# Part of a modulation's column sums moved from VectorE to GpSimd in a one-core transformer kernel

## The chip, the cores and the metric

The kernel runs on one core of a Trainium2 chip. The metric is device microseconds (us) of one execution; lower is better. Three timed runs of the kernel before gave 2441.3, 2444.15 and 2444.39 us, so the median is 2444.15 us.

## The reference, cut to what matters

The reference is three transformer layers on a 256 x 2048 float32 activation. Only the first layer is modulated by a conditioning vector `c` of 2048 numbers:

```
mod = (c @ w_mod + b_mod).reshape(6, 2048)        # w_mod is 2048 x 12288, float32
shift_m, scale_m, gate_m, shift_f, scale_f, gate_f = mod
h    = rms_norm(x, g_pre_mix) * (1 + scale_m) + shift_m
proj = h @ w_in                                    # and so on: mixing, w_out
x    = x + gate_m * rms_norm(mix_out, g_post_mix)
h2   = rms_norm(x, g_pre_ffn) * (1 + scale_f) + shift_f
...
x    = x + gate_f * rms_norm(f, g_post_ffn)
```

The other matrix products are split into a high and a low part in a reduced format (three matmuls for each). The product `c @ w_mod` is different: it is one row times a 100 MB matrix, so it costs little arithmetic and much reading.

## The kernel before, in words

**Weights of the large products.** All matrices come in 1024 KB loads into three buffers `raw`, issued by SyncE's queue (line 130). Each half of a load, 128 x 1024, is split: ScalarE rounds it to `wh` (line 134), VectorE subtracts, `wl = raw - wh` (line 135), and TensorE multiplies with both. There are three `wh` and three `wl` buffers. This happens 802 times and is most of VectorE's work. Both inputs of line 135 lie in SBUF.

**The modulation** is summed over `c`'s 16 chunks of 128 rows. For each chunk, 128 rows of `w_mod` lie on the 128 partitions, and VectorE does `acc = w * c_k + acc` with `c_k` one number per partition (`scalar_tensor_tensor`; the first chunk only multiplies, `tensor_scalar`). At the end TensorE adds the 128 partitions up with a column of ones. It is done in two ways.

*First part: scale_m and shift_m, in `start` (lines 756 to 898).* They are needed before `h` exists. The first 256 columns are done in `first`. The rest goes in four groups (`steps`): columns of chunks 2-3, 4-7, 8-11 and 12-15, that is 256, 512, 512 and 512 columns. For a group, loads of 1024 KB (`raws`, line 769) alternate between scale (segment 1) and shift (segment 0); a load holds 8 chunks of 256 columns or 4 chunks of 512. `mod_part` (lines 777 and 779) adds it up in `macc[:, 0]` (scale) or `macc[:, 1]` (shift). There are three `raws` buffers used in turn, so a load waits until the load three places before it has been used. When both sums are there, TensorE's line 793 adds up the partitions, VectorE's line 800 adds the bias, and lines 808 to 810 make the next chunks of `h` (`xh`, `xl`). `run` weaves the groups into the products with the chunks of `h` that are already there (`pairs(0)`, `pairs(2)`, `full(1)`, `full(2)`), so that a group's chunks are ready two pieces of work before their turn.

*The rest: gate_m, scale_f, shift_f and gate_f, in `mod_tile` (line 446).* It takes tiles of one chunk by 1024 columns (512 KB, line 453, two or three buffers), 96 in the attention block and 32 in the FFN. VectorE's line 457 (first chunk) or 460 adds each in `mac`; the sum over partitions (line 442, by `mod_flush`) is made when the next run of 16 tiles is at its second tile. `side` hands the tiles out at a rate of 3, later 4, for each load of weights.

**What orders the work.** Each engine works through its own list in order. The framework makes the lists at build time from priorities and from its own timing of each instruction. SyncE's queue issues the `raw`, `raws` and `rawm` loads in one list, so a load that waits for its buffer holds up those behind it. GpSimd does almost nothing: sixteen powers of at most two columns and a few small loads.

Of the kernel before, what the change touches and what calls it, by code (L numbers as in the profile page):

```python
# [12 lines left out]
ALU = mybir.AluOpType  # L13
# [3 lines left out]
P = 128  # L17
T = 256
D = 2048
KC = D // P  # L20
# [69 lines left out]
class Kern:  # L90
# [51 lines left out]
    def mm3(self, out, ah, al, bh, bl, start, stop):  # L142
        mm = self.nc.tensor.matmul
        mm(out, ah, bh, start=start, stop=False, skip_group_check=True)  # L144
        mm(out, ah, bl, start=False, stop=False, skip_group_check=True)  # L145
        mm(out, al, bh, start=False, stop=stop, skip_group_check=True)  # L146
# [299 lines left out]
    def mod_tile(self, new, at, k):  # L446

        nc = self.nc

        if k == 1:  # L450
            self.mod_flush()
        raw = new("rawm")
        nc.sync.dma_start(raw, self.A["w_mod"][k * P:(k + 1) * P, at * P:(at + 8) * P])
        cc = self.vcol("c", k)
        if k == 0:
            self.mac = new("mac")
            nc.vector.tensor_scalar(self.mac, raw, cc, None, ALU.mult)
        else:
            dst = self.mac if k < KC - 1 else raw
            nc.vector.scalar_tensor_tensor(dst, raw, cc, self.mac, ALU.mult, ALU.add)  # L460
        if k == KC - 1:
            self.mod_due = (raw, 8, at)

# [292 lines left out]
    def start(self, ps, low, xs, xl, X, sbs, cst):  # L756
        nc, A = self.nc, self.A
# [8 lines left out]
        def mod_load(seg, c0, n, k0, nk):  # L766
            raws.append(raws.pop(0))
            raw = raws[-1]().rearrange("p (k n) -> p k n", k=nk)
            nc.sync.dma_start(raw, wm[:, k0:k0 + nk, seg * D + c0:seg * D + c0 + n])
            return raw  # L770

        def mod_part(acc, raw, k0, n=None):

            for k in range(n or raw.shape[1]):
                cc = self.vcol("c", k0 + k)
                if k0 + k == 0:
                    nc.vector.tensor_scalar(acc, raw[:, k], cc, None, ALU.mult)
                else:
                    nc.vector.scalar_tensor_tensor(acc, raw[:, k], cc, acc, ALU.mult, ALU.add)

        def steps(j0, n):

            macc = ps.tile([P, 2, 512], F32, name="macc", tag="macc", bufs=2)
            nk = 16 // n
            for q in range(0, KC, nk):
                for i, seg in enumerate((1, 0)):
                    mod_part(macc[:, i, :n * P], mod_load(seg, j0 * P, n * P, q, nk), q)
                    yield None
            mp = self.acc("b")
            for i in range(2):  # L790
                for j in range(n):
                    o = i * n + j
                    nc.tensor.matmul(mp[:, o:o + 1], macc[:, i, j * P:(j + 1) * P], self.ones1,
                                     start=o == 0, stop=o == 2 * n - 1, skip_group_check=True)
            yield mp
# [24 lines left out]
        def first():  # L820

            mp = self.acc("b")
            macc = ps.tile([P, 2, 512], F32, name="macc", tag="macc", bufs=2)
            for q in range(0, KC, 8):
                for i, seg in enumerate((1, 0)):
                    if i:
                        raw = self.wp.tile([P, 2048], F32, name="raw", tag="raw", bufs=RAW).rearrange("p (k n) -> p k n", k=8)
                        nc.sync.dma_start(raw, wm[:, q:q + 8, seg * D:seg * D + 2 * P])
                    else:
                        raw = mod_load(seg, 0, 2 * P, q, 8)  # L830
                    mod_part(macc[:, i, :2 * P], raw, q, 6)
                    for k in range(6, 8):
                        for j in range(2):
                            o = 2 * i + j
                            nc.tensor.matmul(mp[:, o:o + 1], raw[:, k, j * P:(j + 1) * P], self.vcol("c", q + k),
                                             start=q + k == 6 and o == 0, stop=False, skip_group_check=True)
            for o in range(4):
                nc.tensor.matmul(mp[:, o:o + 1], macc[:, o // 2, o % 2 * P:(o % 2 + 1) * P], self.ones1,
                                 start=False, stop=o == 3, skip_group_check=True)
            return mp  # L840
# [38 lines left out]
        def run(work, nw, j0, n, lead=2):  # L879

            s = steps(j0, n)
            nm = 2 * n
            done = 0
            for i, _ in enumerate(work):
                while done < nm and done * (nw - lead) < (i + 1) * nm:
                    next(s)
                    done += 1
                if done == nm:
                    chunks(j0, n, next(s))
                    done += 1  # L890
# [582 lines left out]
```

## Time and profile before

| | |
|---|---|
| timed runs, median (lowest, highest) | 2444.15 us (2441.3, 2444.39) |
| profiled execution, its own time | 2438.1 us |
| its span, first to last instruction | 2436.1 us |
| TensorE busy | 2378.1 us, 98% |
| VectorE busy | 1678.5 us, 69% |
| ScalarE busy | 1246.7 us, 51% |
| GpSimd busy | 19.3 us, 1% |

Busy time is the time in which at least one instruction of the engine was in progress. Matmul records are pipelined and their ends are modelled, so TensorE's share says only that it seldom waited. In the views below a stretch is given in us from the span's start; "xN" counts instructions; "idle before" is time the engine stood still just before such instructions, with what released it. `PE` is TensorE, `PEld` its weight loads, `DVE` VectorE, `ACT` ScalarE, `POOL` GpSimd, `SPq` SyncE's queue.

### The profile page before, as it was taken

To read this page: it belongs to the slowest core of one execution; us is meant where nothing else is said; L and a number is where in the kernel's file an instruction comes from. 1 tells how busy PE (TensorE), PEld (TensorE's weight loads), DVE (VectorE), ACT (ScalarE), POOL (GpSimd) and SP (SyncE) were. 2 spreads that over 40 slices of the span, in tenths; PEclk is the share of its full clock that TensorE was granted. 3 is DMA by queue.
4 is the path that set the end of the run, shared out by engine and by line. 5 is a ranking of instruction groups with operands and counts; after the bars stand their busy time and mean duration, and the time that the engine had idled before them with its cause. 6 is when DMAs were issued, how large, how long until landed. Compare 5 with 4: busy or idle time off the path is not lost.

```text
span 2436.1 us, 37172 instructions
## 1 busy us (share of the span) xinstructions
PE 2378.1 (98%) x15142; PEld 2153.9 (88%) x15142; DVE 1678.5 (69%) x2213; ACT 1246.7 (51%) x1716; POOL 19.3 (1%) x30
## 2 busy tenths in 40 slices
PE   7999999999989999999999989999999999999997
PEld 6899989999868888888888879998898899999986
DVE  8997898888777575555556566756664477777764
ACT  5877674534464444444445454445644455554543
POOL 0000000000000000000000000000000000000000
PEclk9999999999999999999999999999999999999999
DMA  9997557999948585555555545555655544454453
GB/s 365 349 365 259 182 177 272 329 350 333 350 161 321 191 291 193 190 189 187 194 197 200 190 149 191 191 189 186 228 193 190 190 163 167 158 189 169 161 190 138
DMA packets 104043, 540.61 MB, mean 222 GB/s; under 512 B 9888, under 2 KB 18240, under 8 KB 53184
## 3 DMA queue, kind: packets, MB, share of 16 engines
q1 hardware_dynamic: 100896, 526.19, 60.8%
q10 hardware_dynamic: 2160, 8.88, 1.0%
q0 software_dynamic: 816, 3.16, 0.4%
q8 instruction: 118, 1.93, 0.3%
q14 instruction: 53, 0.43, 0.1%
HBM read 533.99 MB, written 4.21 MB: 221 GB/s over the span
## 4 chain that ended last, share of the span: by engine, by line
PE 94%; DVE 2%; ACT 1%; DMA 1%; issue 1%; POOL 0%; SPq 0%; DVEq 0%; POOLq 0%
PE acca L145 15%; PE acca L144 15%; PE acca L146 15%; PE acca L212 11%; PE acca L211 11%; PE acca L213 11%; PE acca L193 2%; PE acca L194 2%; PE acca L192 2%; PE accb L212 2%; PE accb L213 2%; PE accb L211 2%; DMA hid<-in_w_mod_dram 1%; DVE wl L135 1%; PE accb L1343 1%
## 5 line engine op out<-in xcount | busy, mean ns | idle before, releaser
L135 DVE TENSOR_TENSOR wl<-raw,wh 128x1024 fp32r<-128x1024 f32 x802 | 977.9, 1221 | 570.9 <-ACT wh L134 568.3
L134 ACT CAST wh<-raw 128x1024 fp32r<-128x1024 f32 x802 | 841.7, 1051 | 864.0 <-PE acca L213 377.9
L145 PE MATMUL acca<-Ql,wh 128*128 128x256 f32 x1024 | 290.5, 284 | 0.0
L144 PE MATMUL acca<-Qh,wh 128*128 128x256 f32 x1024 | 289.8, 284 | 0.0
L146 PE MATMUL acca<-Qh,wl 128*128 128x256 f32 x1024 | 285.5, 281 | 0.0
L212 PE MATMUL acca<-wl,Fh 128*128 128x512 f32 x704 | 276.8, 393 | 1.0 <-DVE wl L135 0.9
L213 PE MATMUL acca<-wh,Fl 128*128 128x512 f32 x704 | 275.7, 393 | 0.3 <-DVE Fl L716 0.3
L211 PE MATMUL acca<-wh,Fh 128*128 128x512 f32 x704 | 252.3, 396 | 1.7 <-ACT Fh L714 1.7
L144 PE MATMUL acca<-xh,wh 128*128 128x256 f32 x832 | 232.8, 284 | 4.5 <-ACT xh L808 3.4
L145 PE MATMUL acca<-xl,wh 128*128 128x256 f32 x832 | 233.7, 284 | 0.0
L146 PE MATMUL acca<-xh,wl 128*128 128x256 f32 x832 | 227.0, 283 | 0.0
L144 PEld LDWEIGHTS acca<-Qh,wh 128*128 128x128 f32 x1024 | 192.9, 188 | 0.5
L145 PEld LDWEIGHTS acca<-Ql,wh 128*128 128x128 f32 x1024 | 192.6, 188 | 0.8
L146 PEld LDWEIGHTS acca<-Qh,wl 128*128 128x128 f32 x1024 | 192.1, 189 | 0.4
L144 PEld LDWEIGHTS acca<-xh,wh 128*128 128x128 f32 x832 | 158.1, 190 | 7.3 <-ACT xh L808 3.6
L145 PEld LDWEIGHTS acca<-xl,wh 128*128 128x128 f32 x832 | 157.4, 189 | 1.6 <-issue 0.7
L212 PEld LDWEIGHTS acca<-wl,Fh 128*128 128x128 f32 x704 | 132.7, 189 | 29.1 <-DVE wl L135 2.2
L211 PEld LDWEIGHTS acca<-wh,Fh 128*128 128x128 f32 x704 | 131.3, 188 | 30.0 <-ACT Fh L714 2.9
L213 PEld LDWEIGHTS acca<-wh,Fl 128*128 128x128 f32 x704 | 132.4, 188 | 28.6 <-DVE Fl L716 1.5
L146 PEld LDWEIGHTS acca<-xh,wl 128*128 128x128 f32 x832 | 155.1, 190 | 1.3 <-issue 1.0
L145 PE MATMUL acca<-Al,wh 128*128 128x256 f32 x512 | 143.7, 282 | 0.0
L144 PE MATMUL acca<-Ah,wh 128*128 128x256 f32 x512 | 142.7, 281 | 0.0
(374 smaller groups left out, 4600.5 us busy)
## 6 DMA issues: line engine op xcount, KB each, us to landing
raw<-in_w_fgu_dram SPq DMA_DIRECT2D x88, 1024.0 KB, 4.8
raw<-in_w_inb_dram SPq DMA_DIRECT2D x64, 1024.0 KB, 4.8
raw<-in_w_in_dram SPq DMA_DIRECT2D x51, 1024.0 KB, 6.3
rawm<-in_w_mod_dram SPq DMA_DIRECT2D x96, 512.0 KB, 5.7
raw<-in_w_fd_dram SPq DMA_DIRECT2D x44, 1024.0 KB, 4.8
raw<-in_w_ina_dram SPq DMA_DIRECT2D x32, 1024.0 KB, 4.8
raws<-in_w_mod_dram SPq DMA_DIRECT2D x30, 1024.0 KB, 8.4
raw<-in_w_in_g_dram SPq DMA_DIRECT2D x16, 1024.0 KB, 7.2
```

The costliest lines, as they stand in the source:

```text
L134: nc.scalar.copy(wh[:, :per], raw[:, a:a + per])
L135: nc.vector.tensor_sub(wl[:, :per], raw[:, a:a + per], wh[:, :per].bitcast(F32))
L144: mm(out, ah, bh, start=start, stop=False, skip_group_check=True)
L145: mm(out, ah, bl, start=False, stop=False, skip_group_check=True)
L146: mm(out, al, bh, start=False, stop=stop, skip_group_check=True)
L192: mm(banks[h], xh[:, t], wh[:, s], start=fresh and k == 0, stop=False, skip_group_check=True)
L193: mm(banks[h], xh[:, t], wl[:, s], start=False, stop=False, skip_group_check=True)
L194: mm(banks[h], xl[:, t], wh[:, s], start=False, stop=k == nk - 1, skip_group_check=True)
L211: mm(banks[h][q], xh[:, t], wh[:, w], start=k == 0, stop=False, skip_group_check=True)
L212: mm(banks[h][q], xh[:, t], wl[:, w], start=False, stop=False, skip_group_check=True)
L213: mm(banks[h][q], xl[:, t], wh[:, w], start=False, stop=k == nk - 1, skip_group_check=True)
L1343: nc.tensor.matmul(ps[:, g * T:(g + 1) * T], q[g][:, P:T], kT, start=g == 0, stop=g == 1, skip_group_check=True)
```

## The change

In `steps` the scale stays with `mod_part` on VectorE, and the shift goes to a new `mod_pool` on GpSimd. It multiplies a whole load (128 x 2048) by `c`, repeated along the columns, in one `tensor_tensor`, and then adds its 4 (or 8) chunks into `macc[:, 1]` with one `tensor_tensor` each. `first` is left as it was. In `mod_tile`, columns 0 to 767 stay on VectorE; columns 768 to 1023 go to GpSimd, as a multiplication by `c_k` in place (`tensor_scalar`) and an addition (`tensor_tensor`), or the multiplication alone for the first chunk.

```
@@ mod_tile
         if k == 0:
             self.mac = new("mac")
-            nc.vector.tensor_scalar(self.mac, raw, cc, None, ALU.mult)
+        dst = self.mac if k < KC - 1 else raw
+        a, b = slice(0, 768), slice(768, 1024)
+        if k == 0:
+            nc.vector.tensor_scalar(dst[:, a], raw[:, a], cc, None, ALU.mult)
+            nc.gpsimd.tensor_scalar(dst[:, b], raw[:, b], cc, None, ALU.mult)
         else:
-            dst = self.mac if k < KC - 1 else raw
-            nc.vector.scalar_tensor_tensor(dst, raw, cc, self.mac, ALU.mult, ALU.add)
+            nc.vector.scalar_tensor_tensor(dst[:, a], raw[:, a], cc, self.mac[:, a], ALU.mult, ALU.add)
+            nc.gpsimd.tensor_scalar(raw[:, b], raw[:, b], cc, None, ALU.mult)
+            nc.gpsimd.tensor_tensor(dst[:, b], raw[:, b], self.mac[:, b], ALU.add)
@@ start
+        def mod_pool(acc, raw, k0):
+
+            n = raw.shape[1]
+            nc.gpsimd.tensor_tensor(raw, raw, self.vcol("c", k0, n)[:, :, None].to_broadcast(list(raw.shape)), ALU.mult)
+            for k in range(n):
+                if k0 + k == 0:
+                    continue
+                nc.gpsimd.tensor_tensor(acc, raw[:, k], raw[:, 0] if k0 + k == 1 else acc, ALU.add)
+
@@ steps
-                    mod_part(macc[:, i, :n * P], mod_load(seg, j0 * P, n * P, q, nk), q)
+                    (mod_part, mod_pool)[i](macc[:, i, :n * P], mod_load(seg, j0 * P, n * P, q, nk), q)
```

## Rows read from the trace of the kernel before

**Rows 1.** The page: the chain that ended last, by engine.

```profile
PE 94%; DVE 2%; ACT 1%; DMA 1%; issue 1%; POOL 0%; SPq 0%; DVEq 0%; POOLq 0%
```

**Rows 2.** Stretches: length, busy by engine, granted clock, DMA share, GB/s.

```profile
28.00:58.00 30.00, 29.95 (x188) 27.15 (x189) 28.49 (x52) 18.92 (x28) 0.00 (x0) 1.00 1.02 376
58.00:98.00 40.00, 37.91 (x270) 34.92 (x268) 36.80 (x51) 39.63 (x67) 0.00 (x0) 0.99 0.97 358
98.00:150.00 52.00, 50.50 (x335) 46.93 (x336) 47.33 (x65) 36.53 (x55) 0.00 (x0) 0.94 0.96 364
150.00:215.00 65.00, 65.00 (x455) 60.60 (x454) 53.06 (x73) 50.45 (x74) 0.00 (x0) 1.00 0.76 278
...
360.00:600.00 240.00, 233.34 (x1940) 231.81 (x1939) 209.58 (x237) 113.77 (x172) 0.00 (x0) 0.99 0.89 322
600.00:660.00 60.00, 60.00 (x275) 50.00 (x274) 46.67 (x47) 25.82 (x33) 1.76 (x3) 1.00 0.94 346
720.00:780.00 60.00, 59.97 (x271) 49.09 (x270) 49.98 (x54) 26.68 (x32) 0.00 (x0) 1.00 0.91 327
```

**Rows 3.** VectorE's groups between 28 and 215 us, shapes apart.

```profile
L135 DVE TENSOR_TENSOR wl<-raw,wh 128x1024 fp32r<-128x1024 f32 x62 | 75.2, 1221 | 17.9 <-ACT wh L134 16.8 <-PE acca L146 0.9
L779 DVE SCALAR_TENSOR_TENSOR macc<-raws,vec,macc 128x512 f32<-128x512 f32 x90 | 65.8, 747 | 1.2
L779 DVE SCALAR_TENSOR_TENSOR macc<-raws,vec,macc 128x256 f32<-128x256 f32 x30 | 13.4, 479 | 0.2
...
L777 DVE TENSOR_SCALAR macc<-raws,vec 128x512 f32<-128x512 f32 x6 | 2.9, 480 | 0.0
```

**Rows 4.** VectorE's groups of the whole span: a tile of the rest.

```profile
L460 DVE SCALAR_TENSOR_TENSOR mac<-rawm,vec,mac 128x1024 f32<-128x1024 f32 x84 | 107.4, 1279 | 10.8 <-DMA rawm<-in_w_mod_dram 10.5
```

**Rows 5.** Stretches, line 460 alone: length, VectorE busy (instructions), clock, DMA share, GB/s.

```profile
360.00:600.00 240.00, 83.56 (x66) 0.99 0.89 322
600.00:660.00 60.00, 16.34 (x14) 1.00 0.94 346
720.00:780.00 60.00, 19.23 (x15) 1.00 0.91 327
```

**Rows 6.** GpSimd in order of time: start, duration, instruction (idle before it).

```profile
246.69 1.72 POOL L313 TENSOR_TENSOR rr<-ms,mhalf 128x2 f32<-128x2 f32 x1 [230.77 <-DVE ms L311]
...
290.91 3.21 POOL L981 TENSOR_TENSOR rsd<-mv,mhalf 128x2 f32<-128x2 f32 x1 [21.25 <-DVE mv L979]
...
686.31 0.57 POOL L260 TENSOR_TENSOR rt<-mst,mhalf 128x1 f32<-128x1 f32 x1 [63.98 <-DVE mst L259]
```

**Rows 7.** VectorE in order of time, beside rows 6.

```profile
246.45 0.16 DVE L311 TENSOR_SCALAR ms<-accb 128x2 f32<-128x2 f32 x1 [0.31 <-PE accb L303]
246.63 1.23 DVE L135 TENSOR_TENSOR wl<-raw,wh 128x1024 fp32r<-128x1024 f32 x1
...
291.22 2.34 DVE L135 TENSOR_TENSOR wl<-raw,wh 128x1024 fp32r<-128x1024 f32 x2
...
686.33 1.24 DVE L135 TENSOR_TENSOR wl<-raw,wh 128x1024 fp32r<-128x1024 f32 x1
```

**Rows 8.** End of the third group: VectorE's last sums, TensorE's sum over partitions.

```profile
142.01 2.32 DVE L779 SCALAR_TENSOR_TENSOR macc<-raws,vec,macc 128x512 f32<-128x512 f32 x3
...
148.03 0.95 PE L793 MATMUL accb<-cst,macc 128*128 128x1 f32 x8
```

**Rows 9.** Waits: TensorE's between 20 and 130 us.

```profile
PE acca L144 <- ACT xh L808: 3.4, 2, 2.6
...
PE acca L144 <- ACT acca L753: 1.0, 1, 1.0
```

**Rows 10.** The page: DMA issues, the last column is us from issue to landing.

```profile
raws<-in_w_mod_dram SPq DMA_DIRECT2D x30, 1024.0 KB, 8.4
```

**Rows 11.** SyncE's queue: first and last of eight such loads of one group.

```profile
103.88 0.37 SPq L769 DMA_DIRECT2D raws<-in_w_mod_dram  x1
...
144.36 0.38 SPq L769 DMA_DIRECT2D raws<-in_w_mod_dram  x1
```

## The prediction

> **What bounds the kernel now.** I first read the busy shares and the chain of waits. TensorE makes up 94% of the chain that ended last, VectorE 2% [rows 1]: time taken off VectorE only counts where TensorE waits for it. Then I cut the span into the stretches that the change touches [rows 2]. The four groups of the first part lie at about 28 to 58, 58 to 98, 98 to 150 and 150 to 215 us, the tiles of the rest mainly from 360 to 660 and from 720 to 780. The reader is to see three things. TensorE is busy for nearly all of each stretch. The DMA engines are full up to 150 us (shares 0.96 to 1.02) and nearly so later (0.89 to 0.94). And VectorE is busy for 28.5 of 30, 36.8 of 40, 47.3 of 52 and 53.1 of 65 us, later for 209.6 of 240, 46.7 and 50.0 of 60. So it has little time left in the very stretches at stake, yet is seldom what TensorE waits for: between 20 and 130 us TensorE's waits for its operands add up to 3.4 + 1.0 = 4.4 us [rows 9].
>
> **What the change removes from VectorE.** In the first part it is the shift's half of the sums between 28 and 215 us [rows 3]: 13.4/2 = 6.7 us in the 256-column group, (65.8 + 2.9)/2/3 = 11.4 in each of the three others. In the rest, a step of 1024 columns takes 1.28 us [rows 4] and one of 512 columns 0.75 [rows 3], which is 1.04 ns a column; 256 columns fewer save 0.27 us a tile.
>
> **What it adds to GpSimd.** A shift load of 2048 columns costs a multiplication over 2048 columns and additions over another 2048: 4096 columns a load, four loads in each 512-column group (16,400 columns), two in the small group (8,200). A tile adds 256 + 256 = 512 columns in two instructions.
>
> **The price of a GpSimd column** is not in this trace, since its instructions have one or two columns. They take 0.57 us where a small one of VectorE's takes 0.16 [rows 6, 7]. The low end is VectorE's 1.04 ns a column. The high end is the ratio of the small ones, 3.6 times, 3.7 ns. In ratio the middle is 1.9 times; I take 1.8 ns, a little below it, because the 3.6 comes from instructions that are all start-up.
>
> **Do the two engines run beside each other?** Everything hangs on this, and the trace has three rows on it. At 246.69 us a GpSimd instruction began just after a VectorE subtraction with two SBUF inputs (246.63, 1.23 us); it took 1.72 us and ended 0.55 us after that subtraction did. At 290.91 one ran into two of these back to back (until 293.56) and took 3.21, ending 0.56 after the second. At 686.31 one began 0.02 us before such a subtraction and took its plain 0.57; the subtraction took 1.24 instead of 1.22 [rows 3, 6, 7]. So GpSimd stands still while VectorE reads two inputs from SBUF. The other direction is open, since a two-column read is over at once. I take it that the exclusion goes both ways: then the time that both need adds up on one port, and what exceeds a stretch lengthens it. If only GpSimd waits, the sum is no other, as the shift is needed at the group's end all the same. The Trainium skill has this as a rule, against the change (SBUF — State Buffer, "Who interferes with whom"): a VectorE instruction with two SBUF inputs and a GpSimd instruction that reads SBUF exclude each other for the whole instruction. By that rule the sum below stands; without it the first rival does.
>
> **The sum, first part.** Per group: VectorE's busy time, minus what is removed, plus GpSimd's columns at 1.8 ns (14.7 us small, 29.5 large), minus the stretch.
> - 28 to 58: 28.5 - 6.7 + 14.7 - 30 = +6.5
> - 58 to 98: 36.8 - 11.4 + 29.5 - 40 = +14.9
> - 98 to 150: 47.3 - 11.4 + 29.5 - 52 = +13.4
> - 150 to 215: 53.1 - 11.4 + 29.5 - 65 = +6.2
>
> Together +41 us. At 1.04 ns it is 0, +2.4, +0.9, 0 = +3; at 3.7 ns about +150. I count every VectorE instruction as holding the port, which is a little too much, and let GpSimd find every gap, which is too kind.
>
> **The sum, the rest.** A tile holds the port for 512 x 1.8 ns = 0.92 us and frees 0.27: +0.65. From 360 to 600 there are 66 such steps [rows 5], +42.9 us, against 240 - 209.6 = 30.4 us of VectorE's idle time [rows 2]: +12.5. From 600 to 660, 14 x 0.65 = 9.1 fits into 13.3, and from 720 to 780, 15 x 0.65 = 9.8 into 10.0. Together +13 us. At 1.04 ns all fits: 0. At 3.7 ns a tile costs 1.62, and it is 76 + 9 + 14, about +100.
>
> **What is queued behind the waits.** A late shift holds TensorE at line 793, with the matmuls behind it, and VectorE at line 800, with the next subtractions behind it. In the third group the last sums ended at 144.3 and line 793 came at 148.0 [rows 8]: 3.7 us are free, and GpSimd needs 5 x 0.57 + 4096 x 1.8 ns = 10.2 us for the last load where VectorE needed about 3. That eats the slack and is part of the sum, not an extra. In `mod_tile` the partition sum of line 442 waits for GpSimd's last addition; it is placed a tile later, which covers about a tile's time. GpSimd's own small powers now stand behind up to two instructions of a tile, under 2 us each, at two or three places; I cost that at nothing, since TensorE's matmuls of the stretch cover it, and at 2 to 4 us if not.
>
> **Total.** 2438.1 + 41 + 13 = 2492 us against the profiled execution. The timed median stands 6 us above that execution, which is inside what the price leaves open, so I don't add it. Where only a page has a price: the GPSIMD Engine Reference of the Trainium skill (Elementwise — side-by-side cycle accounting) gives 4497 ns for a 2048-column float32 addition, 2.2 ns a column; by it I would estimate +64 and +29, 2531 us. No run so far shows it.
>
> **The rivals.**
> *Faster: the engines don't hold each other up* beyond a start. VectorE's relief then counts where TensorE waited for it: the 4.4 us up to 130 us [rows 9]; after that I see no wait of its own for it in these stretches and grant 2 us. 2438 - 6 = 2432 us. For it: no row shows VectorE held up by more than 0.02 us. Against it: GpSimd was held for 1.15 and 2.6 us, and DMA is full up to 150 us, so earlier sums don't bring earlier weights. It decides if a subtraction beside a long GpSimd instruction still takes 1.22 us. Chance 0.13.
>
> *No change: the port is shared, but a GpSimd column costs no more than one of VectorE's.* The sum's low end, +3, falls into the slack: 2441 us, 2444 on the timed runs. For it: both engines move 128 lanes. Against it: the small instructions' 0.57 against 0.16. Chance 0.12.
>
> *Slower for another reason: buffers.* No exclusion, but GpSimd keeps a shift load 10.2 us. Eight loads of the third group were issued over 40.5 us [rows 11], 5.8 us apart, so a buffer of three comes round in 17.4. Landing takes 8.4 [rows 10]; with 10.2 it needs 18.6, and SyncE's queue, with the weights behind it, slips by 0.4 us a load, 3 us a group; in the 40 us group, with loads 5 us apart, 1.2 us a load, 10 us; the small group some 2. 2438 + 15 = 2453 us. For it: DMA has no room to catch up. Against it: the last group has some (share 0.76). Chance 0.15.
>
> That the change doesn't do what it says I leave out: the code moves what it names, and the lists only decide when.
>
> **How the numbers follow.** The forecast, exclusion at about 1.8 ns, has 0.60. Its own range is 2441 to 2570, by prices of 1.04 to 2.6 ns. About 0.2% (5 us) is what a measurement of this kernel can tell from no change. Slower by more: 0.60 + 0.15 = 0.75; within: 0.12; faster: 0.13. The range 2440 to 2570 leaves out the first rival (0.13) and prices above 2.6 ns (0.07).
>
> **What would show it.** Right: between 28 and 215 us, VectorE's subtractions or GpSimd's additions take visibly longer than alone, that part ends 30 to 60 us later, and TensorE waits at line 793 or for `wl`. The 360 to 660 part grows by 10 to 30. A 512-column addition that nothing holds up takes 1.2 to 1.7 us. Wrong: line 135 stays at 1.22 us beside long GpSimd work and the first part ends at the same time (first rival), or only SyncE's waits at line 769 grow (third).

## The result, and the profile after

The changed kernel takes 2531.65 us (median of four runs, 2530.65 to 2542.46) against 2442.91 for the kernel before, timed beside it: 88.7 us more. The ratio over all runs is 1.0375, 95% interval 1.036 to 1.0391 (1.0363 by the two medians). The profiled execution is the longest of the four, 2542.46 us, against 2438.1 before; what is read from the profiles therefore adds up to 104 us where the medians differ by 89.

TensorE bounded the kernel before, so the first thing to read is whether it still does. The page's chain that ended last, by engine, of the kernel after:

```profile
PE 81%; DVE 7%; DMA 4%; POOL 4%; issue 2%; ACT 1%; ACTq 0%; SPq 0%; DVEq 0%; POOLq 0%
```

Against [rows 1], TensorE's share fell from 94 to 81%, VectorE's rose from 2 to 7, and GpSimd, which had 0, has 4. Where this happens shows in the stretches, cut as in [rows 2] (length, busy time of PE, PEld, DVE, ACT and POOL, granted clock, DMA share, GB/s), of the kernel after:

```profile
28.00:58.00 30.00, 22.76 (x113) 20.39 (x114) 27.98 (x27) 11.50 (x18) 21.91 (x17) 0.89 0.76 274
58.00:98.00 40.00, 34.82 (x232) 31.93 (x231) 34.47 (x31) 30.29 (x49) 20.27 (x10) 0.96 0.73 260
98.00:150.00 52.00, 36.77 (x203) 31.38 (x201) 51.05 (x39) 29.50 (x48) 38.68 (x16) 0.87 0.75 269
150.00:215.00 65.00, 47.91 (x309) 44.23 (x310) 59.16 (x41) 31.89 (x47) 47.87 (x23) 0.89 0.67 243
215.00:240.00 25.00, 21.30 (x127) 19.29 (x127) 19.68 (x15) 13.30 (x20) 14.80 (x7) 0.82 0.76 274
360.00:600.00 240.00, 222.75 (x1715) 213.90 (x1714) 201.94 (x293) 121.81 (x197) 127.38 (x91) 0.95 0.71 249
```

VectorE is as busy as before, with fewer instructions: in the third stretch 51.05 us for 39 of them, where it was 47.3 for 65. TensorE lost 13.7 us of 50.5 in that stretch alone, and the DMA share fell from 0.96 to 0.75, so the DMA engines aren't what is short. I took each matmul in the order of both traces and compared its start; the times here are those of the kernel before. The kernel after is 19 us late at 81 us, 45 at 150, 63 at 200 and still 63 at 237, when the first part is over. The tiles in attention add 28: 5 at about 250 us, with the first of them, and 23 more by 720 (91). The tiles in the FFN add some 13.5 (104.5 at 988), and from there to the end less than 1 us is lost.

Why VectorE is busy without doing more is in its groups, the ones of [rows 3] and a small one at line 823, between 28 and 240 us, shapes apart:

```profile
L135 DVE TENSOR_TENSOR wl<-raw,wh 128x1024 fp32r<-128x1024 f32 x49 | 96.1, 1983 | 14.7 <-ACT wh L134 14.7
L793 DVE SCALAR_TENSOR_TENSOR macc<-raws,vec,macc 128x512 f32<-128x512 f32 x41 | 57.9, 1411 | 1.7 <-DMA raws<-in_w_mod_dram 0.9
L793 DVE SCALAR_TENSOR_TENSOR macc<-raws,vec,macc 128x256 f32<-128x256 f32 x15 | 17.0, 1131 | 0.4
L823 DVE TENSOR_SCALAR y<-y,gs 128x256 f32<-128x256 f32 x12 | 13.0, 1102 | 1.3 <-ACT xh L822 1.3
```

The same instruction on the same shape takes 1983 ns instead of 1221, 1411 instead of 747, 1131 instead of 479. (Line 793 is line 779 of before.) The last row has one SBUF input only; it is held up as well, since it took 407 ns in the kernel before, at line 809:

```profile
L809 DVE TENSOR_SCALAR y<-y,gs 128x256 f32<-128x256 f32 x16 | 6.3, 407 | 0.2 <-ACT xh L808 0.2
```

The two engines in order of time, start and duration, of the kernel after:

```profile
29.00 3.74 POOL L780 TENSOR_TENSOR raws<-raws,vec 128x2048 f32<-128x2048 f32 x1 [13.13 <-DVE y L823]
29.19 3.83 DVE L793 SCALAR_TENSOR_TENSOR macc<-raws,vec,macc 128x256 f32<-128x256 f32 x1
...
98.26 14.76 DVE L135 TENSOR_TENSOR wl<-raw,wh 128x1024 fp32r<-128x1024 f32 x5
...
105.13 4.58 POOL L780 TENSOR_TENSOR raws<-raws,vec 128x2048 f32<-128x2048 f32 x1
109.67 13.46 POOL L784 TENSOR_TENSOR macc<-raws,macc 128x512 f32<-128x512 f32 x7
```

At 29 us a step of 256 columns, 0.48 us alone, began 0.19 us after GpSimd's multiplication and ended 0.28 us after it: this is the direction that [rows 6, 7] left open. From 98.26 us five subtractions, 6.1 us alone, took 14.76, and seven additions 13.46. Seven additions alone would take 8.5 us, by the first experiment. GpSimd's groups over the whole span show the same, 1771 ns for an addition of 1220 alone, 1761 for a tensor_scalar of 900:

```profile
L464 POOL TENSOR_SCALAR rawm<-rawm,vec 128x256 f32<-128x256 f32 x90 | 158.3, 1761 | 147.6 <-DMA rawm<-in_w_mod_dram 142.8 <-DVE wl L135 2.4 <-DVE qT L352 2.2
L465 POOL TENSOR_TENSOR mac<-rawm,mac 128x256 f32<-128x256 f32 x84 | 88.7, 1056 | 6.0
L784 POOL TENSOR_TENSOR macc<-raws,macc 128x512 f32<-128x512 f32 x42 | 74.4, 1771 | 3.1
L780 POOL TENSOR_TENSOR raws<-raws,vec 128x2048 f32<-128x2048 f32 x14 | 55.2, 3945 | 76.4 <-DVE macc L793 25.7 <-DMA raws<-in_w_mod_dram 20.6 <-DVE wl L135 16.9
```

TensorE's waits between 28 and 240 us (total, times, longest), the successors of [rows 9]:

```profile
PE acca L146 <- DVE wl L135: 22.9, 9, 9.4
PE acca L193 <- DVE wl L135: 10.2, 3, 4.5
PE acca L145 <- DVE xl L824: 5.4, 2, 3.5
PE accb L807 <- DVE macc L793: 3.4, 1, 3.4
PE accb L807 <- POOL macc L784: 2.3, 1, 2.3
```

TensorE waits for `wl`, hardly for the shift itself (2.3 us). With four smaller waits the list adds up to 49.4 us, 45 more than the 4.4 before. The granted clock bears part of the rest. It fell from the upper level (2.4 GHz) to the lower (1.2) behind such waits: from 116 to 121 us TensorE was busy for only 1.54 us, and from 122 to 135 the granted clock was 0.50. Length times what its mean lacks of 1 is 23.3 us over the five stretches up to 240 us, by the rows above, and was 3.5 in [rows 2]. 45 and 20 make 65, against the 63 us by which the kernel after is late at that point; it is an upper estimate, since a wait at the lower level counts in both.

### The profile page after: what moved, and what is told of

Same layout as the page of the kernel before. It is cut to its first block, busy times and chain, and to the rows that moved or that the text cites. A ratio compares the mean times of both kernels' runs of the same rounds, so it can differ in the third digit from the quotient of the medians.

```text
span 2540.7 us, 37573 instructions
## 1 busy us (share of the span) xinstructions
PE 2415.6 (95%) x15142; PEld 2181.7 (86%) x15142; DVE 1745.9 (69%) x2149; ACT 1245.8 (49%) x1716; POOL 515.2 (20%) x352
## 4 chain that ended last, share of the span: by engine, by line
PE 81%; DVE 7%; DMA 4%; POOL 4%; issue 2%; ACT 1%; ACTq 0%; SPq 0%; DVEq 0%; POOLq 0%
PE acca L145 12%; PE acca L146 12%; PE acca L144 12%; PE acca L212 10%; PE acca L211 10%; PE acca L213 10%; DVE wl L135 3%; DMA hid<-in_w_mod_dram 2%; DVE macc L793 2%; PE acca L193 2%; PE acca L194 2%; PE acca L192 2%; DMA rawm<-in_w_mod_dram 2%; PE accb L212 2%; PE accb L211 2%
## 5 line engine op out<-in xcount | busy, mean ns | idle before, releaser
L135 DVE TENSOR_TENSOR wl<-raw,wh 128x1024 fp32r<-128x1024 f32 x802 | 1039.1, 1299 | 578.0 <-ACT wh L134 572.4
L146 PE MATMUL acca<-xh,wl 128*128 128x256 f32 x832 | 234.5, 289 | 26.4 <-DVE wl L135 26.4
L260 POOL TENSOR_TENSOR rt<-mst,mhalf 128x1 f32<-128x1 f32 x12 | 7.6, 641 | 1131.5 <-DVE mst L258 666.8
L464 POOL TENSOR_SCALAR rawm<-rawm,vec 128x256 f32<-128x256 f32 x90 | 158.3, 1761 | 147.6 <-DMA rawm<-in_w_mod_dram 142.8
```

The source lines that it names most:

```text
L135: nc.vector.tensor_sub(wl[:, :per], raw[:, a:a + per], wh[:, :per].bitcast(F32))
L464: nc.gpsimd.tensor_scalar(raw[:, b], raw[:, b], cc, None, ALU.mult)
```

## The experiments

Two theories at first. **A, the port**: VectorE and GpSimd exclude each other, both ways, while both read SBUF. **B, GpSimd's time**: it is slow, keeps buffers and results too long, and the slower VectorE is beside the point. "The port" is a name for whatever it is that they exclude each other on; an instruction "holds" it for as long as the other engine stands still. All ratios are against the kernel before on the same chip.

**m1_pairs, the prices by themselves.** The kernel's whole computation is left out; blocks of VectorE instructions (two SBUF inputs of 1024 columns; one input from PSUM; one SBUF input) run alone, GpSimd's alone, then both. It is one execution.

```python
("two", 8, None, 0), ..., (None, 0, "add512", 6), (None, 0, "mul2048", 3), (None, 0, "ts256", 6),
("two", 16, "add512", 8), ("two", 16, "mul2048", 4), ("two", 16, "ts256", 8),
("two", 16, "set2048", 8), ("psum", 24, "add512", 8), ("one", 24, "add512", 8)
```

> A kernel of its own: it leaves out the whole computation and runs fifteen blocks, with all engines stopped between two blocks: VectorE alone (two SBUF inputs of 1024 columns; one PSUM and one SBUF input of 512; one SBUF input and a number per partition), GpSimd alone (additions of 512 and 256 columns, the broadcast multiplication of 2048, the multiplication by a number of 256, plain writes of 2048 and 512), and pairs of them at the same time. Theory A, each excludes the other for a whole instruction when both read SBUF through the shared port: 16 two-input subtractions (18.2 us alone) beside 8 additions of 512 columns (about 10 us alone) take about 28 us, beside 4 multiplications of 2048 (about 15 us) about 33 us; beside plain writes, or with VectorE's second input in PSUM, a block takes no more than the longer of the two alone. Theory B, only GpSimd is held up and VectorE never: VectorE's 16 subtractions take 18.2 us in every block. Theory C, no exclusion of long instructions: every pair takes the longer of the two alone.

Measured, a stretch for each block (length, VectorE's busy time and count, GpSimd's, clock, DMA share, GB/s): 8 subtractions alone; 8 of 512 columns with a PSUM input alone; 8 with one SBUF input alone; additions of 512, additions of 256, multiplications of 2048, tensor_scalars of 256 alone; then 16 subtractions beside 8 additions, 4 multiplications, 8 tensor_scalars and 8 pure writes of 2048; 24 with a PSUM input beside 8 additions; 24 with one SBUF input beside 8 additions.

```profile
4.40:13.65 9.25, 9.17 (x8) 0.00 (x0) 1.00 0.00 0
13.70:18.70 5.00, 4.87 (x8) 0.00 (x0) 1.00 0.00 0
18.70:24.30 5.60, 5.39 (x8) 0.00 (x0) 1.00 0.00 0
24.30:31.85 7.55, 0.00 (x0) 7.35 (x6) 1.00 0.00 0
31.85:36.20 4.35, 0.00 (x0) 4.12 (x6) 1.00 0.00 0
36.20:47.10 10.90, 0.00 (x0) 10.71 (x3) 1.00 0.00 0
47.15:52.65 5.50, 0.00 (x0) 5.42 (x6) 1.00 0.00 0
...
62.00:88.90 26.90, 26.77 (x16) 17.70 (x8) 1.00 0.00 0
88.90:120.90 32.00, 31.86 (x16) 18.26 (x4) 1.00 0.00 0
120.90:141.35 20.45, 19.64 (x16) 20.29 (x8) 1.00 0.00 0
141.35:159.75 18.40, 18.25 (x16) 14.02 (x8) 1.00 0.00 0
159.75:174.30 14.55, 14.44 (x24) 9.84 (x8) 1.00 0.00 0
174.30:199.00 24.70, 24.13 (x24) 12.94 (x8) 1.00 0.00 0
```

Sixteen subtractions beside pure writes take 18.25 us, which is twice the eight alone. Beside eight additions they take 8.5 us more, 1.06 for each of 1.22 us; beside four multiplications 13.6 more, 3.40 for each of 3.57. So VectorE stands still for nearly the whole of either: theory A's premise holds. A tensor_scalar of 0.90 us holds it for only 0.17. A PSUM input takes the contention away: 24 at 0.60 us, where eight alone took 0.61 each, and GpSimd's 8 additions in 9.84, their plain 1.23 each. The instruction with one SBUF input doesn't escape: eight alone took 5.39 us, so 24 would take 16.2, and beside 8 additions they take 24.13, 0.99 more for each. Per column GpSimd's multiplication is 1.74 ns (3.57/2048); the addition, between 512 columns (1.22) and 256 (0.69), 2.1.

The Trainium skill has the same line between reads and writes (SBUF — State Buffer, "Who interferes with whom"): two SBUF inputs on VectorE contend with a GpSimd instruction that reads SBUF, not with one that only writes it. The runs agree for `tensor_tensor`. The same page ("Summary: rules for kernel authors") says that the second of the two to issue blocks until the first finishes, which does not fit the tensor_scalar's 0.17 of 0.90 us.

**e1_first_only and e2_rest_only: one part each.** The first undoes `mod_tile`, the second the line in `steps`.

```diff
- (mod_part, mod_pool)[i](macc[:, i, :n * P], ...)     # e2: back to mod_part(...)
- nc.gpsimd.tensor_scalar(raw[:, b], raw[:, b], cc, None, ALU.mult)      # e1: mod_tile
- nc.gpsimd.tensor_tensor(dst[:, b], raw[:, b], self.mac[:, b], ALU.add)
+ nc.vector.scalar_tensor_tensor(dst, raw, cc, self.mac, ALU.mult, ALU.add)
```

> The shift of the first part on GpSimd, the rest's tiles on VectorE alone as before. Theory A (the two parts cost by themselves, the first by exclusion on the port): 2443 + 60 to 70 = 2503 to 2513 us, and the lag stays constant after the first part. Rival (the loss of the first part is made of things the two parts share, such as changed instruction lists): less than 2490 us.

> The first part on VectorE as before, the rest's tiles split 768 to 256 between VectorE and GpSimd. Theory A: 2443 + 30 to 40 = 2473 to 2483 us, about 20 of it in the attention block and about 15 in the FFN. Rival (the rest costs little by itself and only suffers from the first part's delay): under 2455 us.

Measured: 2506.97 us for the first part alone (ratio 1.0271 [1.0255, 1.0286], +65.7) and 2476.03 for the rest alone (1.0158 [1.0137, 1.0179], +34.7). The sum, 100, is a little more than the 88.7 of both. The first part's loss is twice the rest's.

**e3_relief: what the offload could bring at best.** Nothing goes to GpSimd: the shift of the first part isn't summed (its results take the scale's sums), and columns 768 to 1023 of the tiles are left out.

```diff
- (mod_part, mod_pool)[i](...)
+ if i == 0:
+     mod_part(macc[:, i, :n * P], raw, q)
- nc.gpsimd.tensor_scalar(raw[:, b], ...); nc.gpsimd.tensor_tensor(dst[:, b], ...)
```

> VectorE is relieved as in the change but GpSimd does nothing: the shift of the four groups isn't summed (its columns take the scale's sums; its loads are made), and columns 768 to 1023 of the rest's tiles are left out. This is the most that the offload could ever bring. Theory A (VectorE was not what TensorE waited for): 2437 to 2445 us, 0 to 6 us under the kernel before. Rival (VectorE's load was a limit in these stretches, and exclusion hides a real gain): 2430 us or less.

Measured: 2435.78 us, 0.9978 [0.9968, 0.9987]. Even if GpSimd's work cost nothing anywhere, 5.5 us would be all there is to win.

**e4_rest_ffn_third and e5_rest_attention: which tiles of the rest.** From e2, e4 gives the FFN's tiles a third buffer, e5 hands the FFN's tiles back to VectorE.

```diff
- aux = hid[:, 32:44]...; at = {"rawm": [aux[:, 0:1024], aux[:, 1024:2048]], ...}
+ aux = hid[:, 28:44]...; at = {"rawm": [aux[:, 0:1024], aux[:, 1024:2048], aux[:, 3072:4096]], ...}   # e4
- at[name].reverse()
+ at[name].append(at[name].pop(0))
- a, b = slice(0, 768), slice(768, 1024)
+ w = 1024 if at >= 80 else 768; a, b = slice(0, w), slice(w, 1024)        # e5
```

> The kernel with only the rest's tiles split (2476 us), and in the FFN the tiles go through three buffers in place of two (the third is four chunks of the hidden tile that are written only later). Theory A for the FFN (a two-buffer ring: a tile's load waits until GpSimd has done its two instructions one after the other, and the weights wait behind it in SyncE's queue): most of the FFN's 11 us goes, 2463 to 2469 us. Rival (exclusion on the port, as in the first part): within 3 us of 2476.

> The same kernel with the FFN's 32 tiles back on VectorE alone, so only the attention block's 96 tiles are split. Theory A (the parts add): 2476 - 11 = 2465 us, 2462 to 2468. Rival (the FFN's delay comes from work left over by the attention block): 2472 or more.

Measured: 2464.48 us (1.0095 [1.0079, 1.011]) and 2467.23 (1.0102 [1.0087, 1.0118]). They take 12.3 and 9.6 us off e2's +34.7. So the FFN's share, about 11 us, comes by way of the two-buffer ring, and the other 24 us belong to attention (e5 alone has +25.1). The chain of waits in the FFN, of the kernel after (start, duration), shows the ring: load, multiply, add, next load.

```profile
828.61 3.47 DMA hid<-in_w_mod_dram
832.17 1.75 POOL hid L464
833.99 1.14 POOL hid L465
835.14 4.50 DMA hid<-in_w_mod_dram
839.73 1.74 POOL hid L464
```

**e6_first_write and e10_first_write_stt: the same GpSimd time without reads.** Only the first part is moved, and GpSimd writes instead of computing, for as long: two writes in place of a multiplication, three in place of an addition. The shift's sums are left out. e10 adds a change of VectorE's small instruction at line 823 (line 809 before) from one SBUF input to two.

```diff
- nc.gpsimd.tensor_tensor(raw, raw, self.vcol("c", k0, n)..., ALU.mult)
+ for _ in range(2): nc.gpsimd.memset(raw, 0.0)
- nc.gpsimd.tensor_tensor(acc, raw[:, k], ..., ALU.add)
+ for _ in range(3): nc.gpsimd.memset(acc, 0.0)
- nc.vector.tensor_scalar(y, y, scale, shift, ALU.mult, ALU.add)           # e10 only
+ nc.vector.scalar_tensor_tensor(y, y, scale, shift.to_broadcast([P, T]), ALU.mult, ALU.add)
```

> The kernel with only the first part's shift on GpSimd (2507 us), with each GpSimd instruction of it replaced by plain writes to the same tile that take about as long or longer: the multiplication by two writes of 2048 columns (2 x 1.76 = 3.5 us against 3.57), each addition by three writes of 512 (3 x 0.48 = 1.4 against 1.22). The shift's sums are left out by this. Buffers, waits and GpSimd's time stay; only its reading of SBUF is gone. Theory A (exclusion on the shared read port): the loss goes, 2437 to 2450 us. Rival (shift loads kept too long in three buffers, and TensorE waiting for late sums): 2490 us or more.

Measured: 2450.27 us, 1.0026 [1.0, 1.0053], but spread from 2436 to 2461. The mean of line 135 is back at 1222 ns. Two instructions stick out; in order of time, e6:

```profile
57.73 18.49 DVE L820 TENSOR_SCALAR y<-y,gs 128x256 f32<-128x256 f32 x2
...
62.09 4.28 POOL L781 MEMSET macc<- 128x512 f32 x9
66.29 1.82 POOL L776 MEMSET raws<- 128x2048 f32 x1
```

Two tensor_scalars that take 0.4 us each stood for 18.5 us beside GpSimd's row of writes, which is unbroken from 54.84 to 80.77 us. That is contention again, of another pair: one SBUF input against writes. e10 takes it away.

> As e6 (GpSimd only writes, 2436 to 2461 us from run to run), with VectorE's line 809, y * scale + shift, as a scalar_tensor_tensor that reads the shift as a second SBUF input along the columns in place of a tensor_scalar with two numbers per partition. In e6 two of these tensor_scalars took 18.5 us together beside GpSimd's back-to-back writes. Theory A (that instruction uses the shared write side too, and was starved; nothing else of the loss is left): 2436 to 2444 us in all runs. Rival (GpSimd's holding of the buffers costs the 8 us): the median stays at 2448 to 2452.

Measured: 2435.36 us, 0.9977 [0.9964, 0.9989]: the relief of e3, to within half a microsecond. Line 809 wasn't changed by itself in any run, but four of e6's ten runs, without that change, took 2436 to 2439 us as well. VectorE's row and the third stretch of e10:

```profile
L135 DVE TENSOR_TENSOR wl<-raw,wh 128x1024 fp32r<-128x1024 f32 x60 | 72.7, 1221 | 44.1 <-ACT wh L134 43.0 <-PE acca L146 0.7
```

```profile
98.00:150.00 52.00, 51.48 (x352) 47.49 (x351) 36.15 (x44) 39.97 (x60) 41.44 (x56) 1.00 0.96 350
```

GpSimd is busy for 41.44 of these 52 us, more than in the kernel after, in the same buffers, and TensorE loses nothing. GpSimd's own time is not what costs: theory B falls for the first part. What e10 takes away is both sides of the exclusion at once, VectorE's standstill and the time that GpSimd loses to VectorE (1771 ns for an addition of 1220). That TensorE waits for `wl` and hardly for the shift points to the first; no run separates the two.

**e7_rest_write: the same for the rest.** e2 with three writes of 256 columns in place of each GpSimd instruction; columns 768 to 1023 are left out.

```diff
- nc.gpsimd.tensor_scalar(raw[:, b], raw[:, b], cc, None, ALU.mult)
+ for _ in range(3): nc.gpsimd.memset(raw[:, b], 0.0)
- nc.gpsimd.tensor_tensor(dst[:, b], raw[:, b], self.mac[:, b], ALU.add)
+ for _ in range(3): nc.gpsimd.memset(dst[:, b], 0.0)
```

> The kernel with only the rest's tiles split (2476 us), with each of GpSimd's two instructions on a tile replaced by three plain writes of 256 columns (some 0.9 us together, against 0.90 and 0.69); columns 768 to 1023 of the modulation's rest are left out by this. Theory A (in the attention block the port, in the FFN the ring): the attention block's loss goes and the FFN's stays, 2448 to 2458 us. Rival 1 (both are rings): 2470 us or more. Rival 2 (both are the port): 2437 to 2445.

Measured: 2439.72 us, 0.9989 [0.998, 0.9999]: all of e2's loss is gone, the FFN's too. That run's theory A, which left the ring its loss, is wrong, and its rival 2 is right. SyncE's wait for GpSimd before a tile's load, between 700 and 1020 us, in e2, in e7 and in e4:

```profile
SPq L453 <- POOL hid L465: 43.2, 27, 3.3
```

```profile
SPq L453 <- POOL hid L468: 3.9, 8, 0.6
```

```profile
SPq L453 <- POOL hid L465: 51.1, 26, 3.9
```

Held by VectorE, GpSimd's two instructions of an FFN tile take 1.76 + 1.05 = 2.8 us in e2; alone 0.90 + 0.69 = 1.6, and six writes take about 1.9. So a ring of two buffers has room for GpSimd's own time and not for its time under the port. The wait alone is not the cost: e4, with a third buffer and without the FFN's loss, has as much of it. e4 and e7 are two ways out of one cause.

**e8_first_mult and e11_first_mult_quarters: how much port time is free?** From e1, the additions are left out, and the shift's results take the scale's sums; e11 also cuts each multiplication of 2048 columns into four.

```diff
- nc.gpsimd.tensor_tensor(acc, raw[:, k], ..., ALU.add)
+ for k in range(0, n, n // 4):                                            # e11 only
+     r = raw[:, k:k + n // 4]
+     nc.gpsimd.tensor_tensor(r, r, self.vcol("c", k0 + k, n // 4)..., ALU.mult)
```

> The kernel with only the first part's shift on GpSimd (2507 us), with the multiplication of each load kept and its additions left out (the shift's columns take the scale's sums). GpSimd then holds the port for 14 x 3.4 = 48 us in place of about 100. Theory A, a stretch grows only by what exceeds its slack (the prediction's sum, with the measured 3.4 us a multiplication: 28.5 - 6.7 + 6.8 - 30, 36.8 - 11.4 + 13.6 - 40, 47.3 - 11.4 + 13.6 - 52, all below zero): 2440 to 2452 us. Rival, each microsecond of holding costs about as much wherever it falls: half of 66, 2470 us or more.

Measured: 2460.91 us, 1.0076 [1.0057, 1.0095], +19.5: between the two expectations. The forecast's sum, with the multiplications alone at 3.40 us, stays inside every stretch: 36.8 - 11.4 + 4 x 3.40 = 39.0 of 40 us, 49.5 of 52. Its cost would be nothing. VectorE's row between 28 and 235 us of e8:

```profile
L135 DVE TENSOR_TENSOR wl<-raw,wh 128x1024 fp32r<-128x1024 f32 x59 | 88.8, 1524 | 36.9 <-ACT wh L134 34.7 <-PE acca L146 2.1
```

VectorE still had 36.9 us of idle time there, and yet TensorE waited 13.0 us for `wl` at line 146. I took the length of a single hold for the reason, and e11 tests that.

> As the run with the multiplications alone (60 instructions' worth of shift loads, 14 multiplications of 2048 columns, measured at 2460.9 us, 19.5 us over the kernel before), but each multiplication is cut into four of 512 columns. Left out again: the shift's additions. The columns that hold the port are the same, and with a fixed part of 0.2 to 0.3 us an instruction the whole is 0.6 to 0.9 us a load longer. Theory L (the length of one hold is what hurts: VectorE stands still for 3.4 us at a stretch and the subtraction behind it comes too late for TensorE): single holds fall to about 1 us, VectorE's steps come between them, and the time falls to 2450 us or less (under +9). Theory S (the time on the port as a whole is what hurts, however it is cut): 2458 us or more (+17 or more). Between 2450 and 2458: both.

Measured: 2457.52 us, 1.0065 [1.0045, 1.0086], +15, at the upper end of what was expected if both play a part. The holds are short now, 56 of 1.48 us in GpSimd's group, and most of the loss stays:

```profile
L777 POOL TENSOR_TENSOR raws<-raws,vec 128x512 f32<-128x512 f32 x56 | 81.2, 1479 | 105.8 <-DMA raws<-in_w_mod_dram 72.2 <-DVE y L816 13.2 <-DVE wl L135 10.1
```

So my reason was mostly wrong: the length of a hold is worth some 4 us of 19, and as the two intervals overlap, perhaps nothing. The test is not quite even, since four quarters need more time than the whole: the shortest quarter took 1.035 us, four of them 4.1 against 3.57. Either way, time on the port costs before the stretch is full.

**e9_rest_128: half the columns.** From e2, 128 of a tile's columns go to GpSimd.

```diff
- a, b = slice(0, 768), slice(768, 1024)
+ a, b = slice(0, 896), slice(896, 1024)
```

> The kernel with only the rest's tiles split (2476 us), with 128 columns in place of 256 on GpSimd. Theory A (slack): the two instructions hold the port for about 0.45 us a tile and free 0.13, 66 x 0.32 = 21 us against 30 idle in 360 to 600 us: 2440 to 2452 us. Rival (a cost for each tile and instruction, whatever its size: late release of the two or three tile buffers): 2460 us or more.

Measured: 2457.64 us, 1.0064 [1.0049, 1.0079], +16.3, about half of +34.7, between the two expectations. GpSimd's tensor_scalar of 128 columns still takes 1498 ns on average (1783 for 256 in e2), the addition 875 (1042), where the shortest of each took 597 and 452: more than half of their time is waiting, but the loss goes with the columns. By the sum of idle time this load fits (21 us into 30), and yet it costs; the move isn't free at this size either.

No version that computes all the sums beats the kernel before: what e3 allows is 5.5 us, and every one that computed on GpSimd cost more than that.

## Why the prediction was right, and where its terms were off

- **The direction and the mechanism were right.** The exclusion goes both ways (m1, and 29.00 us in the trace), and taking only GpSimd's reads away gives the loss back, in the first part (e10) and in the rest (e7). The time, 2531.65, lies in the range, which is wide, and 40 us above the number: the sizes below were off.
- **The price was right.** I took 1.8 ns a column between 1.04 and 3.7; m1 has 1.74 for the multiplication and 2.1 for the addition. Its durations make 3.57 + 4 x 1.22 = 8.45 us of a large load where I had 7.4, and 18.2 us of the small group where I had 14.7: 3 x 4.3 + 3.5 = 16 us more, if all of it held the port; what the two instructions really hold, 3.40 and 1.06, comes to 7.64 a load. So the price accounts for little of the miss.
- **The first part's term, +41, was mis-sized: +65.7 by e1.** The step that failed is "busy time plus columns minus the stretch", with its zero floor. Matmul by matmul, e1's trace loses 12, 16, 18 and 18 us in the four stretches, where the sum had 6.5, 14.9, 13.4 and 6.2; the miss is largest in the last, which had the most idle time to fill. I called it "too kind" that GpSimd finds every gap, and put no number to it. e8 has the number: where that sum gives nothing, the kernel loses 19.5 us, and 15 with short holds (e11). VectorE's idle time is mostly a wait for `wh`, that is, for TensorE and ScalarE to hand on a buffer; time it spends held just before that can't be made up from idle time after it. That reading fits e8's and e11's rows, but no run moved the idle time by itself. The fallen clock, 20 us by the rows above, was not in the sum; whether it follows only from the waits wasn't tried, though e10, without the waits, has 1.00 in all five stretches.
- **The rest's term, +13, was mis-sized: +34.7 by e2.** For attention, 12.5 stands against some 24, the same failure as above; e9 shows it for the tiles. The price isn't it: by m1 a tile holds VectorE for at most 0.17 + 0.69 = 0.86 us, where I had 0.92. For the FFN I had set 15 x 0.65 = 9.8 us against 10.0 us of idle time and cost it at nothing; it cost about 11. What I overlooked is what is late next: SyncE's load waits for GpSimd in a ring of two buffers (e4, e7). The sum also left tiles out. In e2's trace, matmul by matmul, 6 us are lost at about 250 us, at the first tiles, which I hadn't counted; 21 from 360 to 600; 8 from 720 to 780; and 3 from 840 to 920, at the FFN's other half, which I hadn't counted either.
- **The estimate by the Trainium skill** (GPSIMD Engine Reference, "Elementwise — side-by-side cycle accounting") of +64 and +29, 2531 us, came out almost at the median, by terms that are also near +65.7 and +34.7. It did so with 2.2 ns a column in a sum whose floor was wrong, so the agreement is luck; at the measured durations the first part is +57 by that sum.
- **The rivals.** The first asked for subtractions of 1.22 us beside long GpSimd work: they took 1983 ns. Its gain of 6 us is near the 5.5 of e3, but by luck: in e3's trace the first part, where I had put most of it, ends 8 us later than before, and the gain comes after 215 us. The second needed a column as cheap as VectorE's 1.04 ns. The third, buffers without exclusion, is refuted by e10 and e7, where GpSimd works as long in the same buffers and nothing is lost. (Its eight loads in [rows 11] are not of one group: they are the last five of the third and the first three of the fourth. The third group's own went out from 88.7 to 127.9 us, 5.6 apart, which hardly changes its sum.)
- **What would show it.** The first part ended 63 us later in the trace, not 30 to 60, and the part from 360 to 660 grew by 21, as said; TensorE waited for `wl`, as said, but at the sum over partitions for GpSimd only 2.3 us. The small powers that I cost at nothing don't show in the chain.

## What to carry to other kernels

Ask of a move to GpSimd first what both engines read: where VectorE's main instruction has two SBUF inputs and GpSimd's reads SBUF, the move adds most of GpSimd's time to VectorE's. Here a shift load held VectorE for 7.64 us to spare it 3.0 (four steps of 0.747). Measure beforehand what the relief alone would bring, by leaving the work out: here 5.5 us, against a loss of 89. And don't count an engine's idle time in a stretch as room for more: a third of the loss came in (e8, of e1's) before any stretch was full by its sum.

## What was not expected of the hardware

- Two VectorE tensor_scalars with one SBUF input stood for 18.5 us beside an unbroken row of GpSimd writes (e6), while a subtraction with two SBUF inputs beside writes is not touched (18.25 us for 16, m1). The Trainium skill (SBUF — State Buffer, "Who interferes with whom") says that some VectorE instructions, tensor_scalar among them, can take the pair of ports shared with GpSimd, and then contend with it; the runs agree. That the wait spans more than twenty of GpSimd's instructions, instead of ending with the first, it does not say.
- GpSimd loses time the other way round as well: seven additions of 1.22 us took 13.46 us beside VectorE's row.
- GpSimd's tensor_scalar of 256 columns takes 0.90 us, longer than its addition of two tensors (0.69), and yet it holds VectorE for 0.17 only.
- An input from PSUM on VectorE takes the contention away for both engines (m1). This kernel's `wl` can't use that as it stands, since both of its inputs lie in SBUF.
